# The gate projection by halves of the rows, with the final norm of the first half beside the second half's products

## The chip, the cores and the metric

The kernel runs on one core of a Trainium2 chip. The metric is the device time of one execution in microseconds (us). Three timed runs of the kernel before took 2798.99, 2800.91 and 2802.45 us, median 2800.91 us. The engines are named as in the profile: PE (TensorE), DVE (VectorE), ACT (ScalarE), POOL (GpSimd) and SP (SyncE, which here only issues DMAs); "SPq" and "POOLq" are their queues of DMAs.

## What is computed

The kernel is one inference step of a decoder layer over 576 rows (512 prompt rows and 64 sample rows), width 2048, all in float32. The change touches only the end of it:

```python
def rms_norm(x, g):
    xf = x.astype(jnp.float32)
    y = xf * lax.rsqrt(jnp.mean(xf * xf, axis=-1, keepdims=True) + EPS)
    return (y * g.astype(jnp.float32)).astype(x.dtype)

def finish_layer(x, attn, conv_y, pe, ...):
    ...
    x = x + hid @ w_down
    gate = jax.nn.sigmoid(rms_norm(x, g_ple) @ w_ple_gate)
    return x + (pe @ w_ple) * gate
...
y_prompt = rms_norm(xp, g_final)
y_sample = rms_norm(xs, g_final)
```

So the last stage is one product of 576 x 2048 by 2048 x 2048 (`w_ple_gate`), a sigmoid, a multiplication by `pe @ w_ple` (computed earlier, kept in DRAM as `pl`), the addition of x (kept in DRAM as `x2`), and a final RMS norm over the 2048 features of each row.

## The kernel before

Activations lie with features on the partitions and the 576 rows along the free dimension, so every tensor of width 2048 is eight "pairs" of 128 x 2 x 576. `HR` is 288, half of the rows; `NR` is 576. Each float32 product is made as three products of rounded parts (high by high, high by low, low by high), so every weight and every activation is split into a high part (ACT, a copy, line 149) and a low part (DVE, a subtraction, line 152).

The second phase streams weights in "quads": a quad is a 256 x 256 piece of a weight, four blocks of 128 x 128. `QStream` loads two quads per DMA of 512 KB (line 1625, issued by SP into four buffers `w2r`), and `prep(t + 2)` makes the high part `w2h` and the low part `w2l` of the quad that is used two quads later; each has three buffers. In what follows a *step* is the work of PE on one quad.

The list `segs` in `plan` sets the order of the products. A *segment* is a run of steps that sums one output pair: 32 segments of the up projection (group 1), 40 of the down projection (group 2: each output pair is summed in five parts of 3 to 8 steps, and the last round of eight segments has 8, 8, 8, 7, 6, 5, 4 and 3 steps), then 8 segments of the gate (group 3), one per output pair, 8 steps each. A step of the gate (`plain`) is 24 matmuls of 128 x 128 by 128 x 288: two output blocks, two input blocks, two halves of the rows, three products. I call the boundary between two segments a *seam*.

The gate's activations are x2 itself, scaled by `g_ple` and split: `mk(3, j)` takes a place of the ring `xs` (eight places of 128 x 4032 float32, two in one pool and six in another), and `build` loads pair j of x2 from DRAM on POOL's queue (line 1368), and splits it (lines 149 and 1384). A hook decides at which step each `mk` is recorded: when the place is free (`lastuse`) and x2 of the pair has been finished.

The work behind a segment (`fin_*`) is a generator that `Beside` steps through by a planner's credits: a step gets 2.79 or 3.18 of them, DVE's estimated costs are taken off, and queue 0 (the ends of segments) goes ahead of queue 1 (operands). Program order on each engine is thus fixed when the kernel is built, and each engine executes in order. For a gate segment the work behind it is: four evictions from PSUM, multiplied by the row factor `rb` (`plain_end`, line 1502), the sigmoid (1332), times `pl` (1334), plus `x2` (1336), the square (1240), two additions into the row sum `acc` (1247), a scaled copy by `g_fin` (1341), and a store of the result to DRAM (`x3`, line 1343, POOL's queue) for pairs 0 to 5. `pl` and `x2` are loaded into two buffers `rp` (line 1233, SP) two steps before the seam. Six buffers' worth of results are loaded back near the end (`reload`, line 1412). After the last matmul comes the end of pair 7, then `norm` (row sums on PE, line 173; the reciprocal root by eleven small DVE operations, lines 159 to 164; a diagonal matrix, lines 177 and 179; a product that spreads it over the partitions, line 182; a copy, line 183), then eight multiplications of 128 x 1152 (line 1483) and eight stores of 576 KB (line 1484, SP).

Of the kernel before, what the change touches and what calls it, by code (L numbers as in the profile page):

```python
# [9 lines left out]
F32 = mybir.dt.float32  # L10
# [84 lines left out]
def EL(n):  # L95

    return n / 960.0 + 0.07
# [45 lines left out]
class Kern:  # L143
# [40 lines left out]

    heads = keys = 0
# [4 lines left out]
    def build(self):  # L190
        tc, nc, a = self.tc, self.nc, self.a
        with ExitStack() as top:
            dram = top.enter_context(tc.tile_pool(name="dram", bufs=1, space=DRAM))
            self.am = [dram.tile([128, 2, NR], F32, name=f"am{j}") for j in range(8)]
            self.ypre = [dram.tile([128, NR], F32, name=f"ypre{j}") for j in range(8)]
            self.pl = [dram.tile([128, 2, NR], F32, name=f"pl{j}") for j in range(8)]
            self.x1 = [dram.tile([128, 2, NR], F32, name=f"x1_{j}") for j in range(8)]
            self.x2 = [dram.tile([128, 2, NR], F32, name=f"x2_{j}") for j in range(8)]
            self.x3 = [dram.tile([128, 2, NR], F32, name=f"x3_{j}") for j in range(8)]
# [978 lines left out]

    PRODS = ((0, 2, 0), (5, 6, 4), (6, 5, 5), (4, 4, 3), (1, 3, 1), (2, 0, 2), (3, 1, 6))

    def open2(self):

        tc, nc, es = self.tc, self.nc, self.es2
        P = lambda name, bufs, **k: es.enter_context(tc.tile_pool(name=name, bufs=bufs, reuse_waits="tile", **k))
        self.aux, self.t2, self.w2r, self.w2, self.xsA = (P(n, b) for n, b in (
            ("aux", 1), ("t2", 1), ("w2r", 4), ("w2", 3), ("xsA", 2)))
        self.made = 0
        self.slots = {}
        self.bg = Beside()
        self.fin_of = {}  # L1190
        self.acc2 = self.aux.tile([128, NR], F32, name="acc2")
        self.rb2 = self.aux.tile([128, NR], F32, name="rb2")
        self.plan()
# [14 lines left out]
    def plan(self):  # L1208
# [8 lines left out]
        segs += [(3, p, 0, 8) for p in range(8)]  # L1217
        wsrc = (None, a["w_up"], a["w_down"], a["w_gate"])
        loads = []
        for g, p, k0, k1 in segs:  # L1220
            for k in range(k0, k1, 2):
                m = min(2, k1 - k)
                loads.append((wsrc[g][p][:, k:k + m], m, g == 3))
# [68 lines left out]
    def phase2(self):  # L1292
# [34 lines left out]
        kept = {}  # L1327

        def fin_gate(p, c, r, final):
            for i in (slice(0, 1), slice(1, 2)) if p == 7 else (slice(0, 2),):  # L1330
                ci = c[:, i, :]
                nc.scalar.activation(ci, ci, AF.Sigmoid)
                yield 0
                V(ci, ci, r[0][:, i, :], ALU.mult)
                yield EL(2 * NR)
                V(ci, ci, r[1][:, i, :], ALU.add)
                yield EL(2 * NR)
            yield from self.squares(p, c)
            y = buf("yg") if p < 6 else c
            for i in range(2):  # L1340
                nc.scalar.activation(y[:, i, :], c[:, i, :], AF.Copy, scale=self.g_fin[:, 2 * p + i:2 * p + i + 1])
            if p < 6:
                nc.gpsimd.dma_start(self.x3[p], y)
            else:
                kept[p] = c
            if p == 7:
                yield from self.norm(self.P_)
# [3 lines left out]
               lambda p, final: (pairbuf(self.pl[p]), pairbuf(self.x2[p])))  # L1351

        segs, W, slots, fin_of = self.segs, self.W, self.slots, self.fin_of
        fins = (None, fin_up, fin_down, fin_gate)

        def mk(g, j):

            h = slots[g, j] = Slot()
            t = self.xslot()
            h.hi, h.lo = t[:, 0], t[:, 1]  # L1360
            src = (self.up_in, self.down_in, self.x2)[g - 1][j]
            if g == 3:
                h.hi, h.lo = (x.rearrange("p a n -> p (a n)")[:, :2 * NR].rearrange("p (a n) -> p a n", a=2)
                              for x in (h.hi, h.lo))

# [25 lines left out]
        for t, (si, k) in enumerate(quadlist):  # L1391
            lastuse[segs[si][0], k] = t
# [14 lines left out]
        again = {}  # L1407

        def reload():
            for p in range(6):  # L1410
                y = self.place([128, 2, NR], F32, "y3")
                nc.sync.dma_start(y, self.x3[p])
                again[p] = y

        hook(lastuse[3, 5], reload)
# [7 lines left out]
        for t, (si, k) in enumerate(quadlist):  # L1423
            g, p, k0, k1 = segs[si]
            if prev:
                pg, ppr, c, r, pfinal, pp_ = prev
                if pg == 3:
# [6 lines left out]
                fin_of[pg, pp_] = bg.add(int(late), fins[pg](pp_, c, r, pfinal), 2 if late else None)  # L1434
                before, behind = behind, fin_of[pg, pp_]
                prev = None
            s = slots[g, k]
            if s.work is not None:
                bg.flush(s.work)
                s = slots[g, k]  # L1440
# [4 lines left out]
            if g == 3:  # L1445
                self.plain(pr, hi, lo, s, k == k0, k == k1 - 1)
# [14 lines left out]
            bg.run(1000 + t, 3.18 if g == 3 else 2.79)  # L1461
            if g == 1 and p == 0 and 2 <= k + 2 < 7:
                bg.flush(slots[1, k + 2].work)
            if k == k1 - 1:
# [6 lines left out]
                if g == 3:  # L1471
# [5 lines left out]
        pg, ppr, c, r, pfinal, pp_ = prev  # L1477
        self.plain_end(ppr, c, rb)
        bg.add(0, fins[pg](pp_, c, r, pfinal))
        bg.flush_all(0)  # L1480
        for p in range(8):
            y = kept[p] if p >= 6 else again[p]
            V(y, y, rbb, ALU.mult)  # L1483
            nc.sync.dma_start(a["o_y"][:, 2 * p:2 * p + 2, :], y)

    def plain(self, pr, hi, lo, s, first, last):

        nc = self.nc
        for nh, blocks in enumerate(((2, 3), (0, 1))):
            for kh, ia in enumerate(blocks):  # L1490
                for r in range(2):
# [7 lines left out]
    def plain_end(self, pr, c, rb):  # L1499
        for (nh, r), o in pr.items():  # L1500
            rows = slice(r * HR, r * HR + HR)
            self.nc.vector.tensor_tensor(c[:, nh, rows], o[:, :HR], rb[:, rows], ALU.mult)
        return 4 * EL(HR)
# [184 lines left out]
def layout(inp):  # L1688
# [39 lines left out]
    "o_y": (128, 16, 576), "o_k": (128, 8, 576), "o_v": (128, 8, 576), "o_logf": (128, 5, 8),  # L1728
# [4 lines left out]
def unlayout(r):  # L1733
    y = r["o_y"].transpose(2, 1, 0).reshape(576, 2048)
# [28 lines left out]
```

## Time and profile before

| | |
|---|---|
| median of three runs | 2800.91 us |
| the profiled execution | 2797.89 us |
| its span in the profile | 2796.0 us |
| mean granted PE clock | 0.987 |
| PE busy | 2705.9 us, 97% of the span |
| DVE, ACT busy | 2058.4 us (74%), 1174.4 us (42%) |
| last matmul of the gate starts | 2764.61 us |
| end of the span | 2796.0 us |

The profiled execution lasts 1.89 us longer than its span, and 3.02 us less than the median. A row of the timeline gives the start and the length in us, the engine, the line, the operation, the tile written and those read, and in brackets the idle time before it and what ended that. A row of a view by stretches gives for each stretch the busy time of each engine with the number of instructions, the granted PE clock, the busy share of the DMA engines and GB/s.

### The profile page before, as it was taken

What the parts mean: (1) busy time and instruction counts of PE and PEld (TensorE: products, weight loads), DVE (VectorE), ACT (ScalarE), POOL (GpSimd) and SP (SyncE); (2) the same over time, 40 slices, a digit from 0 to 9 for tenths busy, and PEclk for the clock granted to TensorE, in tenths of its full rate; (3) what the DMA queues carried; (4) which work ended last, traced back from release to release, by engine and by line L of the source; (5) the groups of instructions that cost most, each with busy time, mean ns of one, the idle gap of its engine ahead of it and who ended that gap; (6) DMA issues with size and microseconds to landing.
All of it is one profiled execution on the core that took longest, in us unless ns stands there. A gap on an engine that the chain in (4) does not pass through costs nothing.

```text
span 2796.0 us, 56961 instructions
## 1 busy us (share of the span) xinstructions
PE 2705.9 (97%) x22187; PEld 2609.6 (93%) x22187; DVE 2058.4 (74%) x3613; ACT 1174.4 (42%) x1755; POOL 501.7 (18%) x896
## 2 busy tenths in 40 slices
PE   8999999999989999999999999989999999999996
PEld 7988889898878998999999999989999999999995
DVE  5677777766654346888888888888888888898444
ACT  4233233345634224444444444544444444444332
POOL 1177766731100000000000000100000000000000
PEclk9999999999999999999999999999999999999998
DMA  4688888888735456444444444566565656656444
GB/s 151 200 288 285 280 293 284 295 294 301 254 114 194 139 174 205 130 138 140 135 141 150 140 141 143 195 183 167 151 203 140 180 161 173 179 171 204 154 157 167
DMA packets 232432, 530.81 MB, mean 190 GB/s; under 512 B 25217, under 2 KB 25858, under 8 KB 232162
## 3 DMA queue, kind: packets, MB, share of 16 engines
q1 hardware_dynamic: 167234, 329.72, 36.6%
q0 software_dynamic: 32096, 137.67, 15.6%
q10 hardware_dynamic: 32832, 59.78, 7.0%
q8 instruction: 174, 2.85, 0.4%
q14 instruction: 96, 0.79, 0.1%
HBM read 431.53 MB, written 95.55 MB: 189 GB/s over the span
## 4 chain that ended last, share of the span: by engine, by line
PE 61%; issue 5%; DVE 5%; ACT 1%; DMA 1%; POOL 0%; DVEq 0%; ACTq 0%; SPq 0%; POOLq 0%
PE P L1453 14%; PE P L1452 14%; PE P L1454 14%; PE U L470 8%; PE P L1495 2%; PE P L1496 2%; PE P L1497 2%; PE U L1101 1%; DVE w2l L152 1%; DVE xs L152 1%; DMA w2r<-in_w_down 0%; ACT w2h L149 0%; PE S L723 0%; DVE y L1483 0%; DMA xs<-x 0%
## 5 line engine op out<-in xcount | busy, mean ns | idle before, releaser
L1452 PE MATMUL P<-xs,w2h 128*128 128x288 f32 x3584 | 1065.7, 297 | 17.0 <-DVE c L1543 7.3
L1453 PE MATMUL P<-xs,w2h 128*128 128x288 f32 x3584 | 1064.8, 297 | 4.7 <-DVE xs L152 4.6
L1454 PE MATMUL P<-xs,w2l 128*128 128x288 f32 x3584 | 1060.6, 296 | 2.3 <-DVE w2l L152 2.3
L149 ACT ACTIVATE w2h<-w2r 128x896 fp32r<-128x896 f32 (+1 forms) x576 | 523.5, 915 | 768.9 <-PE P L1453 444.6
L152 DVE TENSOR_TENSOR w2l<-w2r,w2h 128x896 fp32r<-128x896 f32 (+1 forms) x576 | 600.5, 1043 | 205.6 <-ACT w2h L149 204.6
L1452 PEld LDWEIGHTS P<-xs,w2h 128*128 128x128 f32 x3584 | 678.0, 189 | 22.6 <-DVE c L1543 9.7
L1453 PEld LDWEIGHTS P<-xs,w2h 128*128 128x128 f32 x3584 | 678.8, 189 | 7.1 <-DVE xs L152 6.8
L1454 PEld LDWEIGHTS P<-xs,w2l 128*128 128x128 f32 x3584 | 676.7, 189 | 2.7 <-DVE w2l L152 2.7
L470 PE MATMUL U<-xh,whi 128*128 128x288 f32 x1792 | 402.7, 306 | 4.2 <-ACT xh L149 2.8
L470 PE MATMUL U<-xh,wlo 128*128 128x288 f32 x1792 | 385.8, 297 | 3.0 <-DVE wlo L129 3.0
L470 PE MATMUL U<-xl,whi 128*128 128x288 f32 x1792 | 385.0, 297 | 1.2 <-DVE xl L305 1.2
L470 PEld LDWEIGHTS U<-xh,whi 128*128 128x128 f32 x1792 | 289.1, 190 | 25.1 <-issue 16.8
L470 PEld LDWEIGHTS U<-xh,wlo 128*128 128x128 f32 x1792 | 289.7, 190 | 4.1 <-DVE wlo L129 4.1
L470 PEld LDWEIGHTS U<-xl,whi 128*128 128x128 f32 x1792 | 289.7, 190 | 1.7 <-DVE xl L305 1.7
L123 ACT ACTIVATE whi<-wraw 128x512 fp32r<-128x512 f32 x224 | 141.2, 630 | 285.1 <-PE U L470 153.4
L129 DVE TENSOR_TENSOR wlo<-wraw,whi 128x512 fp32r<-128x512 f32 x224 | 160.3, 716 | 102.8 <-ACT whi L123 101.0
L1011 DVE SCALAR_TENSOR_TENSOR y<-ue,cv,y 128x512 f32<-128x512 f32 x240 | 183.3, 764 | 4.2
L1640 DVE TENSOR_TENSOR w2r<-w2r 128x512 f32<-128x512 f32 (+1 forms) x272 | 177.6, 653 | 8.7 <-DMA w2r<-in_w_up 4.4
L1012 POOL TENSOR_SCALAR cvt<-us,cv 128x64 f32<-128x64 f32 x240 | 168.8, 703 | 21.6
L1495 PE MATMUL P<-xs,w2h 128*128 128x288 f32 x512 | 152.2, 297 | 0.1
L1496 PE MATMUL P<-xs,w2h 128*128 128x288 f32 x512 | 151.4, 296 | 0.0
L1497 PE MATMUL P<-xs,w2l 128*128 128x288 f32 x512 | 151.4, 296 | 0.0
(347 smaller groups left out, 2950.3 us busy)
## 6 DMA issues: line engine op xcount, KB each, us to landing
k<-in_cache_kv SPq DMA_DIRECT2D x256, 256.0 KB, 5.1
v<-in_cache_kv SPq DMA_DIRECT2D x256, 256.0 KB, 4.9
w2r<-in_w_up SPq DMA_DIRECT2D x128, 512.0 KB, 4.0
w2r<-in_w_down SPq DMA_DIRECT2D x112, 512.0 KB, 4.2
wraw<-in_w_main ACTq DMA_DIRECT2D x156, 256.0 KB, 5.2
xs<-di POOLq DMA_DIRECT2D x32, 1008.0 KB, 6.0
x<-c POOLq DMA_DIRECT2D x48, 576.0 KB, 5.9
di<-T POOLq DMA_DIRECT2D x32, 576.0 KB, 3.7
```

The source lines that it names most:

```text
L149: self.nc.scalar.activation(out, in_, AF.Copy, **kw)
L152: self.nc.vector.tensor_tensor(out, in_, f(hi), ALU.subtract)
L470: self.nc.tensor.matmul(u[:, r, :HR], w, x[:, r * HR:(r + 1) * HR], start=first and n == 0, stop=last and n == 2)
L1011: nc.vector.scalar_tensor_tensor(y, ue[:, j:j + NPR], w, y, ALU.mult, ALU.add)
L1012: nc.gpsimd.tensor_scalar(t, us[:, :, j:j + 8], w, None, ALU.mult)
L1452: nc.tensor.matmul(o, hi[:, ia, :], s.hi[:, ib, :], start=(k == k0), stop=False)
L1453: nc.tensor.matmul(o, hi[:, ia, :], s.lo[:, ib, :], start=False, stop=False)
L1454: nc.tensor.matmul(o, lo[:, ia, :], s.hi[:, ib, :], start=False, stop=(k == k1 - 1))
L1495: nc.tensor.matmul(o, hi[:, ia, :], s.hi[:, kh, rows], start=first and kh == 0, stop=False)
L1496: nc.tensor.matmul(o, hi[:, ia, :], s.lo[:, kh, rows], start=False, stop=False)
L1497: nc.tensor.matmul(o, lo[:, ia, :], s.hi[:, kh, rows], start=False, stop=last and kh == 1)
L1640: lambda: V(w[:, :, 4:6, :], w[:, :, 0:1, :].broadcast_to([128, m, 2, 128]), w[:, :, 1:3, :], ALU.add),
```

## The change

- The gate's segments are reordered: pair 0 for all rows (group 3), then pairs 1 to 7 for the first 288 rows (group 4), then pairs 1 to 7 for the other 288 rows (group 5): one segment of 24-matmul steps and fourteen of 12-matmul steps. The weights of pairs 1 to 7 are loaded and split twice.
- `rp` of a half segment is one buffer with two parts, filled by two loads of 288 KB (`gate_rows`).
- The work behind a half segment is done on 2 x 288 columns; the credits of its steps are 1.59.
- The results stay on chip: seven pairs of a half fill one place of the ring (`x3`), pair 7 stays in its eviction buffer `c`. The stores to DRAM and the loads back are gone.
- The gate's sixteen operand parts are put three to a place (`unit`), so that six places hold them and two are left for the results. The hooks of `mk(3, j)` change with it.
- When the first half's row sums are complete, `first_half` goes into queue 1: row sums, `half_rsqrt`, a copy, and eight multiplications of 128 x 576 with eight stores of 288 KB on POOL's queue, beside the products of the second half.
- The tail works on 288 rows: the row sums of pairs 0 to 6 are on PE before pair 7's, the squares of pair 7 go to PE directly, the spread factors are read from PSUM without a copy, and the eight stores alternate between SP's and ACT's queues.
- The output `o_y` is laid out as two halves.

```diff
+    def half_rsqrt(self, pt, dg, n, out):
+        ms, rs, t = (self.aux.tile([128, 3], F32, name=x, tag=x) for x in ("hrm", "hrs", "hrt"))
+        nc.vector.tensor_scalar(ms[:96], pt[:96, :6].rearrange("p (a b) -> p a b", b=2)[:, :, 0], 1.0 / n, EPS, ALU.mult, ALU.add)
+        self.rsqrt(None, rs[:96], ms[:96], [96, 3], "", t[:96])
+        nc.vector.tensor_tensor(dg[:96, :HR]..., self.ident..., rs..., ALU.mult)
+        yield
+        o = out()
+        nc.tensor.matmul(o[:, :HR], self.ones[:96, :], dg[:96, :HR], start=True, stop=True)
+        yield o
+    def row_sums(self, pt, x, first, last):
+        for i in range(3):
+            self.nc.tensor.matmul(pt[:96, 2 * i:2 * i + 2], x[:, 96 * i:96 * i + 96], self.ones[:, :2], ...)
...
-        segs += [(3, p, 0, 8) for p in range(8)]
+        segs += [(3, 0, 0, 8)] + [(g, p, 0, 8) for g in (4, 5) for p in range(1, 8)]
...
+        def unit(i):
+            while len(units) <= i:
+                t = self.place([128, 3, 2, NR], F32R, "xs")
+                units.extend(t[:, j] for j in range(3))
+            return units[i]
+        def fin_gate(p, c, r, g):
+            halves = rows_of(g)
+            n = HR * len(halves)
+            c, r = c[:, :, :n], [x[:, :, :n] for x in r]
+            nc.scalar.activation(c, c, AF.Sigmoid)
+            yield 0
+            V(c, c, r[0], ALU.mult)
+            yield EL(2 * n)
+            V(c, c, r[1], ALU.add)
+            yield EL(2 * n)
+            sq = buf("sq2")[:, :, :n]
+            nc.scalar.activation(sq, c, AF.Square)
+            for h in halves:
+                o = (h - halves[0]) * HR
+                for i in range(2):
+                    nc.scalar.activation(x3(p, h, c)[:, i, :], c[:, i, o:o + HR], AF.Copy, scale=self.g_fin[...])
+            yield 0
...
+            if (g, p) == (4, 7):
+                bg.add(1, first_half())
+        def first_half():
+            yield -2
+            pt = self.P_()
+            self.row_sums(pt, self.acc2[:, :HR], True, True)
+            yield -2
+            rs = self.half_rsqrt(pt, self.buf("dg")[:, 0, :], 2048.0, self.P_)
+            next(rs)
+            yield -2
+            nc.scalar.activation(self.rb3, next(rs)[:, :HR], AF.Copy)
+            yield -1
+            for p in (7, 0, 1, 2, 3, 4, 5, 6):
+                y = x3(p, 0)
+                V(y, y, self.rb3[:, None, :].broadcast_to([128, 2, HR]), ALU.mult)
+                nc.gpsimd.dma_start(a["o_y"][0, :, 2 * p:2 * p + 2, :], y)
+                yield EL(2 * HR)
+        def gate_rows(p, g):
+            if g == 3:
+                return pairbuf(self.pl[p]), pairbuf(self.x2[p])
+            r, o = buf("rp"), (g - 4) * HR
+            for i, src in enumerate((self.pl[p], self.x2[p])):
+                nc.sync.dma_start(r[:, :, i * HR:i * HR + HR], src[:, :, o:o + HR])
+            return r[:, :, :HR], r[:, :, HR:]
...
-            at = max(at, lastuse[seq[n - RING]])
+            at = max(at, lastuse[(2, 32 - RING + (2 * j + 1) // 3) if g == 3 else seq[n - RING]])
...
-            bg.run(1000 + t, 3.18 if g == 3 else 2.79)
+            bg.run(1000 + t, (2.79, 3.18, 1.59, 1.59)[max(g - 2, 0)])
...
+        nc.tensor.matmul(pt[:96, :6], self.ones[:, :96], self.none, start=True, stop=False)
+        self.row_sums(pt, acc, False, False)
+        for i in range(2):
+            V(c[:, i, :], ppr[i, 1][:, :HR], rb[:, HR:], ALU.mult)
+            nc.scalar.activation(c[:, i, :], c[:, i, :], AF.Sigmoid)
...
+            y = x3(p, 1)
+            V(y, y, o, ALU.mult)
+            (nc.sync, nc.scalar)[p % 2].dma_start(a["o_y"][1, :, 2 * p:2 * p + 2, :], y)
```

How the instructions stand at three places. First ACT at one seam of the gate: `w2h` are the weights' high parts, `c` is the evicted segment on which the sigmoid works, `sq` the square, `yg` (before) and `x` (after) the scaled result. Before:

```order
L149 ACTIVATE w2h<-w2r 128x512 x7
L1332 ACTIVATE c<-c 128x1152
L1240 ACTIVATE sq_31645<-c 128x1152
L149 ACTIVATE w2h<-w2r 128x512
L1341 ACTIVATE yg<-c,vecs 128x576 x2
L149 ACTIVATE w2h<-w2r 128x512 x7
```

and in the changed kernel:

```order
L149 ACTIVATE w2h<-w2r 128x512 x8
L1375 ACTIVATE c<-c 128x2x288
L1382 ACTIVATE sq_31678<-c 128x2x288
L1386 ACTIVATE x_31387<-c,vecs 128x288 x2
L149 ACTIVATE w2h<-w2r 128x512 x8
```

Sigmoid, square and the two copies stand in one piece now, the next `w2h` behind all of them; before, one `w2h` stood between the square and the copies. So it is at all seven seams behind the first half's segments and at five of the six seams behind the second half's; behind the whole segment of pair 0, and behind pair 2 of the second half, one `w2h` stands between sigmoid and square.

Second DVE at a seam of the gate (`w2l`: the weights' low parts; `acc`: the row sums). Before:

```order
L1502 TENSOR_TENSOR c<-P,rb_12940 128x288 x4
L152 TENSOR_TENSOR w2l<-w2r,w2h 128x512
L1334 TENSOR_TENSOR c<-c,rp 128x1152
L1336 TENSOR_TENSOR c<-c,rp 128x1152
L1247 TENSOR_TENSOR acc_12939<-acc_12939,sq_32923 128x576
L152 TENSOR_TENSOR w2l<-w2r,w2h 128x512
L1247 TENSOR_TENSOR acc_12939<-acc_12939,sq_32923 128x576
```

and after:

```order
L1587 TENSOR_TENSOR c<-P,rb_12932 128x288 x2
L152 TENSOR_TENSOR w2l<-w2r,w2h 128x512
L1377 TENSOR_TENSOR c<-c,rp 128x2x288
L1379 TENSOR_TENSOR c<-c,rp 128x2x288
L1394 TENSOR_TENSOR acc_12931<-acc_12931,sq_31678 128x288
L152 TENSOR_TENSOR w2l<-w2r,w2h 128x512
L1394 TENSOR_TENSOR acc_12931<-acc_12931,sq_31678 128x288
```

The order is the same, with half the columns.

Third POOL's queue where the down projection passes into the gate: `x_n_...<-c` stores pair n of x2, `xs<-x_n_...` loads it as an operand of the gate. Before:

```order
L1322 DMA x_2_91<-c 128x1152
L1368 DMA xs<-x_1_90 128x1152
L1322 DMA x_3_92<-c 128x1152
L1368 DMA xs<-x_2_91 128x1152
L1322 DMA x_4_93<-c 128x1152
L1368 DMA xs<-x_3_92 128x1152
```

and after:

```order
L1343 DMA x_2_91<-c 128x1152
L1443 DMA xs<-x_1_90 128x1152
L1443 DMA xs<-x_2_91 128x1152
L1343 DMA x_3_92<-c 128x1152
L1443 DMA xs<-x_3_92 128x1152
L1343 DMA x_4_93<-c 128x1152
L1443 DMA xs<-x_4_93 128x1152
```

From pair 2 on each load stands right behind the store of the same pair, one segment earlier than before.

More of the change, by code (lines that the diff above doesn't have):

```diff
@@ L1222, in plan @@
                 m = min(2, k1 - k)
[L1223 removed]
+                loads.append((wsrc[g][p][:, k:k + m], m, g >= 3))
         self.segs = segs
@@ L1325, in fin_down, with rows_of @@
                 bg.add(0, self.norm(self.P_))
[L1327 to L1343, printed above, removed]
-            else:
-                kept[p] = c
-            if p == 7:
-                yield from self.norm(self.P_)
+        def rows_of(g):
+            return {3: (0, 1), 4: (0,), 5: (1,)}[g]
@@ new lines, in phase2, with x3 @@
+        units, y3 = [], {}
+        def unit(i):
[3 more added lines that the diff above has]
+            return units[i]
+        def x3(p, h, c=None):
+            if not y3:
+                for i in range(2):
+                    t = self.place([128, 7, 2, HR], F32, "x3")
+                    y3.update({(j, i): t[:, j] for j in range(7)})
+            if p == 7:
+                y3.setdefault((p, h), c)
+            return y3[p, h]
@@ L1490, in plain @@
             for kh, ia in enumerate(blocks):
-                for r in range(2):
+                for r in halves:
                     if first and kh == 0:
```

90 lines of the change are left out of this document (54 added, 36 removed).

## The prediction

> **What bounds the kernel now.** I read the stretches of the gate stage first, then the timelines of PE, ACT and DVE around one of its seams, then DMA issues, then the tail. Three stretches (span; PE, PEld, DVE, ACT and POOL busy; granted clock; DMA share; GB/s):
>
> ```profile
> 2585.40:2764.70 179.30, 179.30 (x1347) 179.27 (x1345) 77.28 (x111) 60.27 (x85) 3.21 (x6) 1.00 0.49 160
> 2764.70:2780.40 15.70, 5.25 (x16) 3.20 (x14) 7.95 (x23) 4.11 (x6) 0.00 (x0) 0.65 0.01 2
> 2780.40:2796.00 15.60, 0.00 (x0) 0.00 (x0) 10.21 (x8) 0.00 (x0) 0.00 (x0) 0.50 0.76 303
> ```
>
> Seven of the gate's eight segments (first row) are PE alone: no gap, DVE 43% and ACT 34% busy. The tail (the other rows, 31.3 us) has no matmul of the gate: first a chain of small operations, then multiplications and stores at 303 GB/s. So the change has 31 us to win from, and anything that makes PE wait in the gate stage adds to the time in full.
>
> PE's pace there, at the seam that I use as a clock; T is the start of the new segment's first matmul, 2738.74:
>
> ```profile
> 2738.61 0.29 PE L1497 MATMUL P<-xs,w2l 128*128 128x288 f32 x1
> 2738.74 0.30 PE L1495 MATMUL P<-xs,w2h 128*128 128x288 f32 x1
> ```
>
> Matmuls start every 0.133 us, so a step of 24 lasts 3.2 us and one of 12 will last 1.6 us. PE's order within a step is high weight, high weight, low weight. ACT and DVE at this seam:
>
> ```profile
> 2739.21 0.63 ACT L149 ACTIVATE w2h<-w2r 128x512 fp32r<-128x512 f32 x1 [2.57 <-PE P L1496]
> 2739.83 1.17 ACT L1332 ACTIVATE c<-c 128x1152 f32<-128x1152 f32 x1
> 2743.82 1.17 ACT L1240 ACTIVATE sq<-c 128x1152 f32<-128x1152 f32 x1 [2.82 <-DVE c L1336]
> 2744.89 0.61 ACT L149 ACTIVATE w2h<-w2r 128x512 fp32r<-128x512 f32 x1
> 2745.41 1.43 ACT L1341 ACTIVATE c<-c,vecs 128x576 f32<-128x576 f32 x2
> ```
>
> ```profile
> 2738.94 0.86 DVE L1502 TENSOR_TENSOR c<-P,rb 128x288 f32<-128x288 f32 x2 [0.74 <-PE P L1497]
> 2739.87 0.69 DVE L152 TENSOR_TENSOR w2l<-w2r,w2h 128x512 fp32r<-128x512 f32 x1
> 2741.03 1.36 DVE L1334 TENSOR_TENSOR c<-c,rp 128x1152 f32<-128x1152 f32 x1 [0.47 <-ACT c L1332]
> 2742.43 1.36 DVE L1336 TENSOR_TENSOR c<-c,rp 128x1152 f32<-128x1152 f32 x1
> ```
>
> The first `w2h` starts at T+0.47, when PE has let its buffer go, and its `w2l` is done at T+1.82; both are for step 2 of the segment. Then ACT takes the sigmoid, waits 2.82 us for DVE, squares, and only then makes the `w2h` of step 3: done at T+6.8. PE wants it at T+9.6 (three steps of 3.2). The seam is covered by 2.8 us, and only because steps are long.
>
> **The change, part by part.**
>
> *Twelve seams between half segments.* A step is 1.6 us, so PE wants the high weights of step 3 at T+4.8 and the low ones at T+5.07. What stands ahead of them on ACT is now the whole end of the segment. Durations for half the columns: DVE's 576-column rows are 0.75 against 1.36 (second row of the tail's DVE fence below), a ratio of 0.55; the same ratio gives 0.65 for sigmoid and square, and two copies of 288 columns take half of 1.43, some 0.75 with their fixed part. The chain: `w2l` of step 1 keeps DVE until T-1.6+1.82 = T+0.22; two evictions, 0.86, T+1.08; sigmoid T+1.75; multiplication T+2.53; addition T+3.30; square T+3.98; copies T+4.73; `w2h` of step 3 T+5.36; its `w2l` T+6.08. PE's third matmul of step 3 starts 1.0 to 1.1 us late. Step 4's parts follow at T+7.1 against a need at T+7.7 (6.67 and the delay), so the loss isn't repeated within the segment, and it isn't regained: PE has no slack.
>
> The loads of `pl` and `x2` can make it worse. Before:
>
> ```profile
> 2730.99 0.37 SPq L1625 DMA_DIRECT2D w2r<-in_w_gate  x1
> 2731.41 0.46 SPq L1233 DMA_DIRECT2D rp<-pl  x1
> 2731.96 0.38 SPq L1233 DMA_DIRECT2D rp<-x  x1
> ```
>
> ```profile
> w2r<-in_w_gate SPq DMA_DIRECT2D x28, 512.0 KB, 4.5
> rp<-pl SPq DMA_DIRECT2D x8, 576.0 KB, 6.1
> rp<-x SPq DMA_DIRECT2D x8, 576.0 KB, 7.2
> ```
>
> They stand behind a weight load on SP's queue. The weights land 4.5 us after issue, `x2` 0.97+7.2 = 8.2 us after the weights' issue: 1152 KB more in 3.7 us. Now it is 576 KB more, 1.8 us, so `x2` lands 6.3 us and `pl` 5.4 us after the weights' issue. That issue waits for the `w2l` of the segment's last step but, by the pace above, T-4.8+1.82 = T-2.98. `pl` lands at T+2.5 (wanted at T+1.78), `x2` at T+3.4 (wanted at T+2.55): up to 0.85 us more. Per seam 1.1 (loads in time) to 1.95 us (loads as worked out); I take the middle, 1.5, because the landing column holds medians of mixed traffic: 12 x 1.5 = +18.0 (13.2 to 23.4). The thirteenth seam of this kind, where a `w2h` stands between sigmoid and square, has its parts at T+4.8 and costs nothing to 0.8.
>
> *The seam behind the whole segment of pair 0.* Here the full-width rows apply, and the sigmoid is preceded by a table load, as before:
>
> ```profile
> 2586.46 1.28 ACT L1332 ACT_TABLE_LOAD   x1
> ```
>
> In order after the step's `w2h` (T+1.1): table load T+2.4, sigmoid T+3.6, multiplication and addition T+6.35, `w2l` of step 3 T+7.05: 2.0 us late. Square T+7.5, four copies T+9.0, `w2h` T+9.55, `w2l` of step 4 T+10.3, against T+8.7 (6.67 and the 2.0): another 1.6. Before, the same chain was hidden by steps of 3.2 us. +3.6.
>
> *What waiting does to PE's pace.* The end of the down projection shows it:
>
> ```profile
> 2534.72 0.40 PE L1452 MATMUL P<-xs,w2h 128*128 128x288 f32 x1 [0.72 <-ACT c L1542]
> 2534.95 0.29 PE L1453 MATMUL P<-xs,w2h 128*128 128x288 f32 x1
> 2535.09 0.29 PE L1454 MATMUL P<-xs,w2l 128*128 128x288 f32 x1
> ...
> 2536.87 0.40 PE L1452 MATMUL P<-xs,w2h 128*128 128x288 f32 x1 [1.10 <-DVE c L1543]
> ```
>
> and the chain of waits just behind:
>
> ```profile
> 2538.05 0.24 PE P L1453
> ...
> 2540.93 0.16 PE P L1453
> ```
>
> After the wait of 0.72 us matmuls go on at 0.13 us. After a second one of 1.10, 1.8 us idle within 2.5, they start 0.24 us apart for some 3.4 us, which costs 3.4 x (1 - 0.133/0.24) = 1.5 us. The seam of pair 0 idles 3.6 us in about 5: +1.5. A seam of 1.5 us, in two pieces, every 13 lies between the two rows; I charge +0.8 in all (0 to 18). The Trainium skill, "TensorE: Matmul & The Clock Gate", section "HAM oscillation — how this bites in real kernels", gives the rule of no PE-idle gaps above about 3.4 us. By that rule neither kind of seam would slow PE and the sum would be 2.3 us lower; the rows above show it after far shorter gaps, so I go by them.
>
> *The tail.* PE and DVE of before:
>
> ```profile
> 2764.61 0.29 PE L1497 MATMUL P<-xs,w2l 128*128 128x288 f32 x1
> 2771.15 2.29 PE L173 MATMUL P<-ones,acc 128*128 128x2 f32 x10 [6.25 <-DVE acc L1247]
> 2776.64 2.07 PE L182 MATMUL P<-dg,ones 128*128 128x512 f32 x2 [3.20 <-DVE dg L177]
> ```
>
> ```profile
> 2764.54 0.86 DVE L1502 TENSOR_TENSOR c<-P,rb 128x288 f32<-128x288 f32 x2 [0.74 <-PE P L1497]
> 2765.31 0.75 DVE L1334 TENSOR_TENSOR c<-c,rp 128x576 f32<-128x576 f32 x1
> ...
> 2773.48 0.17 DVE L175 TENSOR_SCALAR rrm<-P 128x5 f32<-128x5 f32 x1 [2.38 <-PE P L173]
> ...
> 2775.89 0.69 DVE L177 TENSOR_TENSOR dg<-ident,rrs 128x512 f32<-128x512 f32 x1
> ...
> 2780.37 7.70 DVE L1483 TENSOR_TENSOR y<-y,rb 128x1152 f32<-128x1152 f32 x6 [3.63 <-ACT rb L183]
> ```
>
> From the last matmul's start to the span's end it is 31.4 us. Now, from that start: last eviction 0.8, four operations of 288 columns at 0.43 (half of 0.86) 2.5, square 3.0, three row sums of 0.23 3.7, the twelve small DVE operations 6.1 (2773.48 to 2775.89 is 2.4), the diagonal at 288/512 of 0.69 6.5, its product at 288/512 of 2.07 7.7, no copy; eight multiplications of 0.75, 13.7; then the landing of the last store. Before, the last multiplication ended at 2790.6 and the span 5.4 us later with 576 KB per store; with 288 KB between 2.7 and 5.4, so 16.4 to 19.1. I take 17.2, near the lower end, since two queues share half the bytes: -14.2 (-12.3 to -15.0).
>
> *The first half's norm beside products.* On PE three row sums (0.7) and a product of 288 columns (1.2 at the tail's slow pace, half at full): +1.3. On DVE the small operations and the diagonal, 2.8 us in one piece, where a step's `w2l` has 3.47-1.82 = 1.65 us to spare: up to +1.2. The eight multiplications, 6.0 us, fall into one segment of 12.8 us in which DVE has 8 x 0.69 + 0.86 + 2 x 0.75 + 2 x 0.43 = 8.7 us already: 1.9 over, partly within the lookahead. Together +2.5 (1 to 4). POOL's queue is free by then; its 2.4 MB compete with the loads, which is in the 1.95.
>
> *Weights twice, results kept, places.* The weight loads go from 512 KB per 6.4 us to per 3.2 us, 160 GB/s; with `rp` some 210, under the 303 of the tail's stores, and a load is issued 6 steps (9.6 us) ahead of use and lands in 4.5: nothing. The dropped stores and reloads were on POOL's and SP's queues beside PE: nothing. Operands placed three to a place move one split ahead of the down projection's end, and out of the segment that holds the two waits above. If those waits and the slow pace go, -3.3; if the extra split makes a like one later, +3.3; I take +0.5.
>
> **Sum**: 18.0 + 3.6 + 1.5 + 0.8 - 14.2 + 2.5 + 0.5 = +12.7 on the profiled execution's 2797.89 (span 2796.0 and 1.89 around it): 2810.6. That execution is 3.0 below the median of the runs shown, so beside the median: 2813.6.
>
> **Rivals.**
>
> *The seams are covered and the change is faster.* For it: DVE and ACT are less than half busy in the stage, and the chain's hops could be shorter than I add them. The place is `w2h` of step 3; it decides at a loss of about 0.45 us per seam (12.7/12 = 1.06 less than 1.5), that is if step 3's parts come by T+5.5 instead of T+6.1 to T+6.9. With none at those twelve seams: 2813.6 - 18.8 = 2795; with the pair-0 seam covered too, 2790. Against it: every term of the chain is a row, and ACT works in order.
>
> *PE slows down after every seam.* If 1.5 us in two pieces is enough, 12 x 1.5 = 18 in place of the 0.8: 2831.
>
> *The down projection's end decides.* Waits there by ten us either way would need several like those shown; with the bounds above, 2810 to 2816; with the slow pace at two seams, 2818.
>
> **How the numbers follow.** A measurement of this kernel tells some 0.2% (5.6 us) from no change, that is 2795.3 to 2806.5. Chances: forecast 0.60 (2803 to 2822, of it 0.06 below 2806.5), covered seams 0.19 (0.14 faster, 0.05 same), slow PE 0.13, down projection 0.08 (0.02 same). So faster 0.14, same 0.13, slower 0.73. The range leaves out the fastest covered cases and the worst of slow PE: 2796 to 2828; the forecast's own range is 2803 to 2822.
>
> **What would show it.** In the profile after: at each seam a PE wait of 0.5 to 1 us for `w2h` on ACT and one for `w2l` on DVE about 5 us behind the eviction, the square waiting for the addition and the addition for `rp`; PE busy below the stage's length by some 20 us; the granted clock under 1.00 behind the seam of pair 0 only; 17 us from the last matmul to the end. I am wrong if the gate stage lasts within 8 us of before's, if the tail takes over 20 us, or if PE's clock falls at every seam.

## The result, and the profile after

The kernel after the change takes 2829.45 us (median of four runs, 2821.47 to 2833.56). The kernel before, on the same chip, takes 2801.68 us. The ratio is 1.0094, with a 95% interval from 1.0077 to 1.0111: slower by 27.8 us by the medians and by 26 us by the ratio (22 to 31). The forecast was 2813.6 with a range up to 2828, so the sign was right and the size was not.

The profiled execution of after is the longest of its four, 2833.56 us with a span of 2831.5. Against before's profiled execution that is 35.5 us of span, more than the medians differ; the sums below explain the 35.5, since only profiled executions can be taken apart.

By stretches, the thirteen half segments behind the first one, and the tail, in the columns of the prediction's first fence:

```profile
2607.30:2814.10 206.80, 183.96 (x1258) 177.75 (x1257) 116.55 (x202) 89.23 (x156) 4.56 (x8) 0.93 0.54 172
2814.10:2831.50 17.40, 3.52 (x24) 2.44 (x23) 9.87 (x26) 2.60 (x6) 0.00 (x0) 0.64 0.37 136
```

Thirteen segments of 12.8 us should last 166.4 us; they last 206.7. PE is idle for 23 us of it, and the granted clock is 0.93 where before's was 1.00. The tail went from 31.4 us (last matmul's start to the end) to 17.4. What PE waits for in those thirteen segments, with totals, number of waits and the longest:

```profile
PE P L1579 <- ACT w2h L149: 14.9, 12, 2.5
PE P L1581 <- DVE w2l L152: 7.9, 12, 5.7
```

At eleven of the thirteen seams PE waits once for a high part and once, for some 0.2 us, for a low part, as the prediction had it; at one it waits only for a high part, and at one for a low part, for 5.7 us, which the prediction did not have. The seam behind pair 2 of the first half, the one with a high part's wait alone, where the new segment's first matmul starts at T = 2620.94; first DVE, then ACT:

```profile
2620.71 0.89 DVE L1587 TENSOR_TENSOR c<-P,rb 128x288 f32<-128x288 f32 x2
2621.68 0.69 DVE L152 TENSOR_TENSOR w2l<-w2r,w2h 128x512 fp32r<-128x512 f32 x1
2624.32 0.76 DVE L1377 TENSOR_TENSOR c<-c,rp 128x576 f32<-128x576 f32 x1 [1.95 <-DMA rp<-pl]
2625.11 0.76 DVE L1379 TENSOR_TENSOR c<-c,rp 128x576 f32<-128x576 f32 x1
...
2627.99 0.69 DVE L152 TENSOR_TENSOR w2l<-w2r,w2h 128x512 fp32r<-128x512 f32 x1 [0.91 <-ACT w2h L149]
```

```profile
2621.63 0.69 ACT L1375 ACTIVATE c<-c 128x576 f32<-128x576 f32 x1
2625.90 0.68 ACT L1382 ACTIVATE sq<-c 128x576 f32<-128x576 f32 x1 [3.58 <-DVE c L1379]
2626.49 0.94 ACT L1386 ACTIVATE x<-c,vecs 128x288 f32<-128x288 f32 x2
2627.35 1.65 ACT L149 ACTIVATE w2h<-w2r 128x512 fp32r<-128x512 f32 x3
```

This is the forecast chain: the multiplication waits for `pl`, the square for the addition, and the `w2h` of step 3 stands behind square and copies. It starts at T+6.41, where PE wants it done at T+4.8. And PE behind it:

```profile
2628.01 0.61 PE L1579 MATMUL P<-xs,w2h 128*128 128x288 f32 x1 [2.17 <-ACT w2h L149]
...
2629.14 0.44 PE L1579 MATMUL P<-xs,w2h 128*128 128x288 f32 x1
2629.38 0.44 PE L1580 MATMUL P<-xs,w2h 128*128 128x288 f32 x1
...
2631.06 0.40 PE L1581 MATMUL P<-xs,w2l 128*128 128x288 f32 x1
2631.29 0.29 PE L1579 MATMUL P<-xs,w2h 128*128 128x288 f32 x1
2631.42 0.30 PE L1580 MATMUL P<-xs,w2h 128*128 128x288 f32 x1
```

After the wait of 2.17 us the matmuls start 0.24 us apart or more until 2631.29, then 0.13 again. Such stretches at the slow pace, of 9 to 16 matmuls, stand behind six of the thirteen seams (behind pair 7 of the first half the row sums stand in the middle and make it two): 88 slow matmuls, each 0.107 us late.

The 5.7 us wait is at the seam behind pair 2 of the second half. POOL's queue is given the eight stores of the first half from 2726.10 to 2733.49, and SP's the two loads of `rp` behind six of them. POOL, SP and DVE there, and the DMA issues from 2718 to 2745:

```profile
2726.10 0.74 POOL L1413 DMA_DIRECT2D o_y<-c  x1 [153.16 <-DVE c L1412]
...
2733.49 0.54 POOL L1413 DMA_DIRECT2D o_y<-x  x1 [0.73 <-DVE x L1412]
```

```profile
2731.75 1.21 SPq L1422 DMA_DIRECT2D rp<-pl  x1
2733.01 0.75 SPq L1422 DMA_DIRECT2D rp<-x  x1
```

```profile
2734.45 0.68 DVE L152 TENSOR_TENSOR w2l<-w2r,w2h 128x512 fp32r<-128x512 f32 x1
2741.49 0.76 DVE L1377 TENSOR_TENSOR c<-c,rp 128x576 f32<-128x576 f32 x1 [6.35 <-DMA rp<-pl]
2742.28 0.76 DVE L1379 TENSOR_TENSOR c<-c,rp 128x576 f32<-128x576 f32 x1
2742.96 0.69 DVE L152 TENSOR_TENSOR w2l<-w2r,w2h 128x512 fp32r<-128x512 f32 x1
```

```profile
rp<-x SPq DMA_DIRECT2D x1, 288.0 KB, 9.1
```

The `pl` that was issued at 2731.75 holds DVE up until 2741.49, and the `w2l` of step 3, behind the addition on DVE, is what PE waits for.

The tail, PE and DVE:

```profile
2814.06 0.30 PE L1581 MATMUL P<-xs,w2l 128*128 128x288 f32 x1
...
2820.64 1.33 PE L195 MATMUL P<-dg,ones 96*128 96x288 f32 x2 [2.86 <-DVE dg L191]
```

```profile
2822.00 4.74 DVE L1567 TENSOR_TENSOR x<-x,P 128x576 f32<-128x576 f32 x7 [1.42 <-PE P L195]
2826.66 0.75 DVE L1567 TENSOR_TENSOR c<-c,P 128x576 f32<-128x576 f32 x1
```

Where the 35.5 us are, by the starts of matmuls in the two timelines: the gate starts 3.45 us later (2560.60 against 2557.15) and its first segment lasts 0.4 less; the first half segment lasts 18.87 in place of 12.8, +6.1; the other thirteen +40.3; the tail -13.95.

### The profile page after: what moved, and what is told of

The parts are those of the page before. It is cut to its first block, busy times and chain, and to the rows that moved or that the text cites. A ratio compares the mean times of both kernels' runs of the same rounds, so it can differ in the third digit from the quotient of the medians.

```text
span 2831.5 us, 57355 instructions
## 1 busy us (share of the span) xinstructions
PE 2728.6 (96%) x22203; PEld 2628.2 (93%) x22203; DVE 2100.6 (74%) x3715; ACT 1212.2 (43%) x1841; POOL 501.7 (18%) x899
## 5 line engine op out<-in xcount | busy, mean ns | idle before, releaser
L149 ACT ACTIVATE w2h<-w2r 128x896 fp32r<-128x896 f32 (+1 forms) x632 | 556.0, 889 | 767.0 <-PE P L1519 470.1
L152 DVE TENSOR_TENSOR w2l<-w2r,w2h 128x896 fp32r<-128x896 f32 (+1 forms) x632 | 638.0, 1012 | 200.9 <-ACT w2h L149 199.9
L1579 PE MATMUL P<-xs,w2h 128*128 128x288 f32 x512 | 159.1, 311 | 16.1 <-ACT w2h L149 16.1
```

Source lines behind the costliest of these rows:

```text
L149: self.nc.scalar.activation(out, in_, AF.Copy, **kw)
L152: self.nc.vector.tensor_tensor(out, in_, f(hi), ALU.subtract)
L1579: nc.tensor.matmul(o, hi[:, ia, :], s.hi[:, kh, rows], start=first and kh == 0, stop=False)
```

## The experiments

The theory after the comparison: the seams cost what they cost because the first steps' weight parts stand behind the segment's end in program order, and that end in turn waits for loads; and the longer waits slow PE down besides. The rivals: the late loads alone are the cause; the order alone; weights loaded and split twice; the moved operand splits.

**The loads earlier.**

```diff
-            if k == k1 - 2 and not slow:
+            if k == k1 - (4 if g >= 4 else 2) and not slow:
```

> The loads of `pl` and `x2` of a half segment are issued four steps ahead of the seam in place of two, 3.2 us earlier; nothing else changes. Theory A: DVE's waits for these loads (18.6 us in the profile of after) make the seams' idle time long enough to slow PE, so both go together: DVE waits for `rp` under 2 us, the thirteen half seams cost 0.8 us each in place of 3.1, and the time falls by 20 to 28 us against after, to 2801 to 2809. Rival B: the order on ACT and DVE costs most of it and PE slows at any seam: the waits for `rp` go, but the slow runs stay (some 100 matmuls at 0.24 us), and the time falls by 5 to 12 us, to 2817 to 2824. Rival C: the loads are slow because of the traffic and simply land as late as before: within 4 us of after.

Measured: 2806.66 us (ten runs, 2800.33 to 2811.65) beside 2801.21 for before, ratio 1.0024 (1.0011 to 1.0037). In the time that is theory A. DVE's waits for `rp` in the thirteen segments fall from 18.6 us to one of 3.0 (under 2 was expected), at the seam with the stores, and 12 slow matmuls are left of 88, at the same seam. What is left at a usual seam is short; PE behind pair 3 of the first half:

```profile
2639.37 0.29 PE L1581 MATMUL P<-xs,w2l 128*128 128x288 f32 x1
2639.86 0.40 PE L1579 MATMUL P<-xs,w2h 128*128 128x288 f32 x1 [0.20 <-ACT w2h L149]
2640.10 0.29 PE L1580 MATMUL P<-xs,w2h 128*128 128x288 f32 x1
2640.59 0.40 PE L1581 MATMUL P<-xs,w2l 128*128 128x288 f32 x1 [0.20 <-DVE w2l L152]
```

Two waits of 0.20 us. But from 2639.37 to 2640.10 two matmuls take 0.73 in place of 0.27: the wait of 0.20 loses 0.46. The matmul that resumes lasts 0.40 instead of 0.29 and the next starts 0.24 behind it. So each wait costs about 0.27 us beside its own length. Such a seam costs 0.93 in all: evictions follow each other every 13.57 us here, and every 12.64 in the run with both edits below.

**The order.** In `fin_gate`, the part behind a `yield -1` is recorded one split later, so that one `w2h` and one `w2l` go between sigmoid and multiplication, and another pair between addition and square.

```diff
             nc.scalar.activation(c, c, AF.Sigmoid)
-            yield 0
+            yield -1
             V(c, c, r[0], ALU.mult)
             yield EL(2 * n)
             V(c, c, r[1], ALU.add)
-            yield EL(2 * n)
+            yield -1
```

> One split of a later step is recorded between sigmoid and multiplication, and one between addition and square, of every gate segment; the loads stay where they are. So the high weights of step 3 no longer stand behind the whole end of the segment on ACT, while the low weights of step 3 still stand ahead of or between the operations on DVE. Theory A (late loads are what matters): the seams whose loads come late still wait, but for less, since DVE has already made one low part more: the time falls by 15 to 25 us against after, to 2805 to 2815, and waits of DVE for `rp` remain near 18 us in the trace. Rival B (the order is the cause): PE's waits at the seams nearly vanish, under 4 us in all, and with them the slow runs: the time falls by 30 to 38 us, to 2792 to 2800.

Measured: 2796.19 us (ten runs, 2790.01 to 2802.36), ratio 0.9987 (0.9975 to 0.9998): rival B, though not quite as told. PE's waits in the thirteen segments are 4.7 us, and 4.0 of them are the seam with the stores:

```profile
PE P L1581 <- DVE w2l L152: 4.7, 2, 4.0
```

DVE's waits for `rp` did not stay near 18 us but fell to 6.6: with a `w2l` ahead of it the multiplication comes later, and PE no longer loses time in which the loads would land anyway.

**Both edits.**

> Both edits: the loads four steps ahead, and one split of a later step between sigmoid and multiplication and one between addition and square. Both theories expect PE without waits at the seams from pair 1 on and without slow runs: the gate stage within 5 us of before's, the tail at 17.4 us, so 2788 to 2797, faster than before. Rival C (weights loaded and split twice are the cost, through DMA traffic or through DVE and ACT): PE still waits 15 us or more in the stage and the time stays above 2806.

Measured: 2791.29 us (eight runs, 2785.52 to 2797.86), ratio 0.9970 (0.9956 to 0.9983): faster than before, as both theories had it. The gate stage is 5.7 us longer than before's, where at most 5 was expected. In the thirteen segments PE waits once:

```profile
PE P L1581 <- DVE w2l L152: 0.7, 1, 0.7
```

There is no slow stretch of matmuls behind the first half segment. The evictions of the seven half segments of the first half are 12.64 us apart, although the weights of pairs 1 to 7 are loaded and split twice. So that part of the change costs PE nothing there, and rival C falls. The two edits overlap: alone they take 0.0070 and 0.0107 off the ratio, together 0.0124. Each alone removes the long waits at all seams but the one with the stores, so those waits needed both the late loads and the order; neither is their cause by itself.

**The operands' hooks.**

```diff
-            at = max(at, lastuse[(2, 32 - RING + (2 * j + 1) // 3) if g == 3 else seq[n - RING]])
+            at = max(at, lastuse[seq[n - RING]])
```

> After, but the rule that says at which step an operand part of the gate is made is that of before (the place that is reused is taken to be one part to a place). The seams of the gate are left alone. Theory: the profile of after starts the gate 3.45 us later than before's because of two waits of 0.78 and 1.66 us and 16 slow matmuls at the end of the down projection, which the moved splits make; with the old rule these go and the time is 3 us lower than after. Rival: the waits there come from the places being freed later, so a part recorded earlier waits for its place and holds up the splits behind it: same or up to 10 us slower than after.

Measured: 2825.58 us (four runs, 2822.53 to 2829.86), ratio 1.0100 (1.0081 to 1.0120) against after's 1.0094. The time does not tell it from after, and the 3 us less that were expected can't be seen in it. The trace does tell: from the first eviction of the third segment of the down projection's last round to the first of the gate it is 101.46 us in before, 105.61 in after and 101.61 here. The rows for before, after and this run, in this order:

```profile
2482.07 0.45 DVE L1543 TENSOR_TENSOR c<-c,P 128x288 f32<-128x288 f32 x1
...
2583.53 0.46 DVE L1502 TENSOR_TENSOR c<-P,rb 128x288 f32<-128x288 f32 x1
```

```profile
2480.95 0.45 DVE L1628 TENSOR_TENSOR c<-c,P 128x288 f32<-128x288 f32 x1
...
2586.56 0.46 DVE L1587 TENSOR_TENSOR c<-P,rb 128x288 f32<-128x288 f32 x1
```

```profile
2475.82 0.45 DVE L1628 TENSOR_TENSOR c<-c,P 128x288 f32<-128x288 f32 x1
...
2577.43 0.46 DVE L1587 TENSOR_TENSOR c<-P,rb 128x288 f32<-128x288 f32 x1
```

The earlier splits cost 4.1 us there, by more waits than before had. In after the last two are these, with 16 slow matmuls behind the second:

```profile
2548.95 0.40 PE L1518 MATMUL P<-xs,w2h 128*128 128x288 f32 x1 [0.78 <-ACT c L1627]
2551.67 0.41 PE L1518 MATMUL P<-xs,w2h 128*128 128x288 f32 x1 [1.66 <-DVE c L1628]
```

**Both edits and the old hooks.** The three diffs above together.

> The run with both edits of the seams, and besides the old rule for when an operand part of the gate is made. From the evictions of the down projection's last round to the end of the gate's first segment it was 105.6 us in after, 101.5 in before and 101.6 with the old rule alone. Theory: the two effects add, so the time is 4 us below that with both edits, 2787 (2785 to 2789). Rival (the earlier start only moves the next wait, since the same splits are then made beside the gate's first segments): within 1.5 us of it, 2790 to 2793.

Measured: 2788.37 us (four runs, 2785.00 to 2790.83) beside 2802.26 for before, ratio 0.9951 (0.9935 to 0.9968). The median is 1.4 us above the theory's figure and 2.9 below that of the run with both edits; the ratios differ by 0.0019, 5 us, with intervals that overlap. The stretch named above is 101.4 us here and 105.5 in the run with both edits. So the effects add in the trace, and the time speaks for it without settling it.

**Whole segments for more pairs.**

```diff
-        segs += [(3, 0, 0, 8)] + [(g, p, 0, 8) for g in (4, 5) for p in range(1, 8)]
+        segs += [(3, p, 0, 8) for p in range(5)] + [(g, p, 0, 8) for g in (4, 5) for p in range(5, 8)]
```

> As the run before it, but pairs 0 to 4 are done for all rows (whole segments), and only pairs 5 to 7 by halves, so the weights of three pairs are read twice in place of seven. Theory S (what is left is the seam between the whole segment of pair 0 and the first half segment, 6.3 us over its 12.64 with both edits, and it is dear because steps are short behind it while sigmoid's table load, 1152-column operations and the row factor's last part stand ahead): behind pair 0 a whole segment now follows, whose 3.2 us steps cover it as in before; the seam from pair 4 to the first half segment costs 2 to 4 us (no table load), so the time is 2 to 5 us lower than the run before it, 2782 to 2785. Theory W (reading and splitting weights twice costs something by itself): more than that, down to 2778. Rival: the norm of the first half now falls into the first of three half segments with less room, and the time is the same or higher.

Measured: 2785.72 us (four runs, 2783.53 to 2791.88), ratio 0.9945 (0.9927 to 0.9964). It can't be told from the run before it by the time. In the trace the seam from the whole to the half segments went as theory S says: between the first evictions of the two it is 16.1 us here and 19.1 there, and one wait of more than 0.2 us is left:

```profile
2695.61 0.40 PE L1579 MATMUL P<-xs,w2h 128*128 128x288 f32 x1 [1.17 <-ACT w2h L149]
```

The gate from its first eviction to the last segment's first is 2.2 us shorter (184.4 against 186.6). This is the fastest of the kernels tried, 0.55% faster than before.

**The first half's stores.**

```diff
                 V(y, y, self.rb3[:, None, :].broadcast_to([128, 2, HR]), ALU.mult)
-                nc.gpsimd.dma_start(a["o_y"][0, :, 2 * p:2 * p + 2, :], y)
+                if p == 7:
+                    nc.gpsimd.dma_start(a["o_y"][0, :, 2 * p:2 * p + 2, :], y)
```

> After, with seven of the eight stores of the first half's result left out (the products and the norm are all there; the first half of the output is not written but for one pair). Theory: these stores, 2.4 MB on another queue, hold up the loads of `pl` and `x2` for the seam behind pair 2 of the second half, whose multiplication waited 6.35 us and PE 5.7 us: that wait of PE falls to 0.5 to 2 us, the other seams stay, and the time falls by 4 to 7 us against after, to 2822 to 2826. Rival: those loads are late through their own queue and place behind a weight load; PE's wait there stays over 4 us and the time within 2 us of after.

Seven of the eight stores are left out here, so most of the first half's output is not written. Measured: 2822.22 us (four runs, 2821.92 to 2824.57), ratio 1.0071 (1.0055 to 1.0088), 0.0023 or 6.4 us less than after's, with intervals that overlap; the trace is clearer. At the seam behind pair 2 of the second half PE's wait is now

```profile
2736.75 0.40 PE L1582 MATMUL P<-xs,w2l 128*128 128x288 f32 x1 [0.44 <-DVE w2l L152]
```

in place of 5.72. The other seams wait about as in after (18.9 us in all, against 17.1 there). So it was the stores on POOL's queue that held up loads on SP's. They need not cost anything: with the loads four steps ahead and the order changed, the stores are all there and PE doesn't wait at this seam.

**PE's pace behind one idle stretch.** In the kernel before:

```diff
+        (8, 9, 10, 11, 9, 10, 11, 12, 10, 9, 11, 10, 12, 9)[2 * p - 2 + k // 5] if g == 3 and p and k in (2, 5) else 0
...
-        self.k.split_lo(lo, w, hi)
+        for _ in range(1 + again):
+            self.k.split_lo(lo, w, hi)
```

> The kernel before, in which the subtraction for one low weight part is done 8 to 12 times more in the third and the sixth step of gate segments 1 to 7 (the same result is written again), so that PE waits once, for 0.5 to 4 us, at fourteen places a good 9 us apart, with nothing else changed. It measures what one idle stretch of PE does to its pace. Theory T (a threshold): every stretch above some length between 1.1 and 2.2 us is followed by matmuls 0.24 us apart, none below it. Theory W (a window that runs on its own): of stretches of 1.2 to 2.6 us some are followed by slow matmuls and others of the same length are not; below 1 us none, above 3.4 us all. In both a slow run lasts 2 to 5 us. Rival: a single stretch never slows PE below 3.4 us, and only two or more close together do. The time is 20 to 45 us above before.

Measured: 2863.92 us (one run), 61.7 above before. The fourteen stretches and the matmuls 0.24 us apart behind each, from the timeline of PE, by length:

| idle, us | 0.88 | 1.24 | 1.24 | 1.96 | 1.96 | 2.03 | 2.69 | 3.04 | 3.16 | 3.42 | 3.77 | 4.17 | 4.86 | 5.79 |
|---|---|---|---|---|---|---|---|---|---|---|---|---|---|---|
| slow matmuls | 0 | 0 | 0 | 15 | 14 | 0 | 24 | 15 | 14 | 21 | 11 | 11 | 18 | 18 |

Two stretches of nearly one length, the first without and the second with a slow stretch of matmuls:

```profile
2673.76 0.40 PE L1497 MATMUL P<-xs,w2l 128*128 128x288 f32 x1 [2.03 <-DVE w2l L152]
2674.00 0.29 PE L1495 MATMUL P<-xs,w2h 128*128 128x288 f32 x1
2674.13 0.30 PE L1496 MATMUL P<-xs,w2h 128*128 128x288 f32 x1
...
2685.57 0.40 PE L1497 MATMUL P<-xs,w2l 128*128 128x288 f32 x1 [1.96 <-DVE w2l L152]
2685.81 0.29 PE L1495 MATMUL P<-xs,w2h 128*128 128x288 f32 x1
...
2686.44 0.44 PE L1496 MATMUL P<-xs,w2h 128*128 128x288 f32 x1
2686.68 0.44 PE L1497 MATMUL P<-xs,w2l 128*128 128x288 f32 x1
...
2689.56 0.32 PE L1497 MATMUL P<-xs,w2l 128*128 128x288 f32 x1
```

That is theory W, not T, and a single stretch is enough.

The granted clock in the traces shows what decides. In this run it falls to 0.50 ten times in the gate stage, for 3.41 us or for 6.83, and all its changes are whole multiples of 3.41 us apart: they lie on a grid that runs on whatever PE does. Four intervals of this grid, two around the wait of 2.03 us, then two around the wait of 1.96 us, in the columns of the prediction's first fence:

```profile
2669.13:2672.54 3.41, 2.60 (x20) 2.36 (x18) 3.24 (x6) 0.63 (x1) 0.00 (x0) 1.00 0.29 120
2672.54:2675.96 3.42, 2.20 (x16) 2.20 (x17) 2.33 (x4) 0.00 (x0) 0.00 (x0) 1.00 0.12 29
2682.78:2686.20 3.42, 1.46 (x11) 1.22 (x10) 3.32 (x6) 0.63 (x1) 0.00 (x0) 1.00 0.00 0
2686.20:2689.61 3.41, 3.41 (x17) 3.41 (x16) 1.44 (x3) 0.00 (x0) 0.00 (x0) 0.50 0.77 216
```

The grid cuts the wait of 2.03 us in two, 0.8 and 1.2 us of PE's idle time (3.41 less the first figure behind the length), and the clock stays at 1.00. The wait of 1.96 us lies in one interval, and the next has half the clock. So PE's idle time within one interval of the grid counts, not the length of one wait. In the ten traces, from 2300 us to the end, a full-clock interval with 1.9 us idle or more was followed by half the clock in 32 of 32 cases, one with less than 1.45 us in none of 1337, and one in between in 17 of 23. After's seams with waits of 1.52, 1.64 and 2.32 us are such cases in between, with 1.71, 1.83 and 1.85 us in one interval; the first two lost the clock, the third did not, and no run tells why.

The stretches became up to 5.8 us long where 4 was meant, hence the time above the 45 told: 40.2 us of idle time, 161 slow matmuls at 0.107 (17.2) and fourteen resumptions at 0.27 (3.8) make 61.2.

## Why the prediction was right and wrong

**The mechanism of the seams was right.** The order on ACT and DVE behind each seam, the wait of the multiplication for `pl`, and the two waits of PE are all in the trace, and two edits that touch nothing else turn the ratio from 1.0094 to 0.9970.

**"Twelve seams between half segments", +18.0: right in its sum, partly by luck.** PE's waits in the thirteen segments are 22.8 us; without the 5.7 at the seam with the stores 17.1 are left, 1.4 a seam where 1.5 was charged. The two parts of it are off. With the loads in time PE waits 0.4 us a seam (0.93 with what resuming costs), where 1.1 was worked out; the late loads add the other 1.0, where 0 to 0.85 was. The 1.1 comes in part from a misreading: T is not the start of a segment. The gate's last matmul starts at 2764.61 and its segment has 192 of 0.133 us, so that segment starts at 2739.14, and 2738.74 is a matmul of the one before. PE's needs thus come 0.40 us later against the chain than told: 1.1 becomes 0.7.

**"What waiting does to PE's pace", +0.8 for all seams but pair 0's: this step failed.** It has two missing parts. The 88 slow matmuls cost 9.4 us. The step charged a mean seam, 1.5 us in two pieces, but the waits are not alike: half of the twelve seams wait about 1.0 in all or less and are not followed by a slow stretch of matmuls; the others wait 1.7 to 2.7, and five of those six are. The rows that were used, 0.72 and 1.10 us, lie on the safe side of the lengths of the table above, and the pair of them slowed PE: they fall into one interval of the clock's grid, which held 1.78 us of idle time. The prediction expected a granted clock under 1.00 behind the seam of pair 0 only; it fell behind six more. And each wait costs 0.27 us when PE resumes, 6.5 us for 24 waits. The prediction quoted rows that show it (0.40 us for the resuming matmul against 0.29) and charged nothing for it.

**The thirteenth seam, "costs nothing to 0.8", and the stores, "which is in the 1.95": failed.** This seam lost 5.7 us of idle time, and the run without the stores shows that they are the cause. Bytes over the stage were the wrong measure: 2.4 MB were issued within 7.4 us, most of them just ahead of the one pair of loads that could not wait; its `x2` part landed 9.1 us after issue, where the median is 5.1.

These make the thirteen segments: 17.1 + 5.7 + 9.4 + 6.5, and some 1.3 for the first half's matmuls, 40.0 of the 40.3 measured. The prediction had 18.0, 0.8 and 2.5 there, 21.3.

**"The first half's norm beside products", +2.5: right as far as it can be seen.** In the run with both edits the three segments in which it lies take 40.8 us against 38.4.

**"The seam behind the whole segment of pair 0", +3.6 and +1.5 for the pace: near.** 6.1 measured; PE waits 1.6 and 1.2 us there. The two edits help little here (6.3 us between evictions are left over the usual 12.64), and a whole segment behind it, more.

**"Operands placed three to a place", +0.5 (-3.3 to +3.3): wrong side.** It is 3.05 us of the 35.5 (3.45 - 0.4), 4.1 by the marks used above. The waits moved one split ahead and grew, and took the slow pace with them; the old rule takes it back.

**"The tail", -14.2: right.** -13.95 measured, 17.4 us where 17.2 was forecast.

The rival "PE slows down after every seam" gave 2831, close to the time, but not by what happened: slow stretches of matmuls stand behind six of thirteen seams, and over half of the missing 19 us is the resumptions and the stores. The rival "the seams are covered" gave 2790 to 2795 and is what the kernel does once they are.

## What to carry to other kernels

When a step is made shorter, the work that stands between two steps on an in-order engine must shrink as well or be spread between them; what covered it before was the length of the step. Issue the loads that such work needs by time, not by steps: "two steps ahead" was halved with the step. And count the waits of PE and how they lie together, not their sum alone: each has a price for resuming, and where some 1.5 to 1.9 us of idle time or more fell into one interval of 3.41 us, the next could run at half the clock.

## What the runs showed of the hardware

- PE's granted clock changes on a grid of 3.41 us that runs on by itself. From 2300 us on it fell to 0.50 behind every full-clock interval in which PE was idle for 1.9 us or more (32 of 32, in ten traces) and behind none with less than 1.45 us (0 of 1337).
- In the table of fourteen idle stretches, one of 0.88 to 1.24 us was never followed by slow matmuls (three of three), of 1.96 to 2.03 in two of three, of 2.69 us and above always (eight of eight). In that table a slow stretch lasts 11 to 24 matmuls of 0.24 us, which costs 1.2 to 2.6 us. In after a seam with 2.32 us was not followed by one and seams with 1.52 and 1.64 were. The Trainium skill, "TensorE: Matmul & The Clock Gate", section "What's actually happening", says that the clock is set by a window of 3.4 us that runs freely; that equal stretches differ agrees with it, and so does the grid. The rule in its section "HAM oscillation — how this bites in real kernels", no gaps above about 3.4 us, does not hold here: 1.96 us was enough.
- A wait of PE costs about 0.27 us beyond its length (0.20 us of waiting lost 0.46).
- A load of `rp` of half the size landed in 5.1 us (median in after), of the full size in 6.9 (before), and its issue on SP took 0.53 and 0.60 us (medians for `pl` and `x2`) in place of 0.46 and 0.37: half the bytes are far from half the time, though the weights' traffic beside them differs.
- The evictions of the first half's segments are 12.64 us apart where PE doesn't wait, those of the second half 12.80. No run tells why.
